# First loads and last norm of a two-layer encoder kernel: pieces alternated, a product halved, six multiplications moved to GpSimd

## The chip, the cores and the metric

The kernel runs on one core of one Trainium2 chip. The metric is the device time of one execution in microseconds (us). The time before is the median of 3 runs. A profile of one execution goes with it. The engines are named as in the profile: PE (TensorE; PEld is its weight load), DVE (VectorE), ACT (ScalarE), POOL (GpSimd) and SP (SyncE, which only issues transfers here). A q behind an engine's name is its queue of transfers.

## What is computed

The reference is a two-layer encoder on 512 tokens of width 1024. Each layer adds a half-weighted SwiGLU network, then two gated mixers (neighbourhood attention and a Fourier mix), then a second half-weighted SwiGLU network; a final RMSNorm ends it.

```
def rms_norm(x, g):
    y = xf * lax.rsqrt(jnp.mean(xf * xf, axis=-1, keepdims=True) + RMS_EPS)
    return y * g

def swiglu(x, w_in, w_out):
    g, u = jnp.split(x @ w_in, 2, axis=-1)
    return (jax.nn.silu(g) * u) @ w_out

for l in range(DEPTH):
    x = x + 0.5 * swiglu(rms_norm(x, ffn1_norm[l]), ffn1_w_in[l], ffn1_w_out[l])
    x = x + mixer(rms_norm(x, mix_norm[l]), ...)
    x = x + 0.5 * swiglu(rms_norm(x, ffn2_norm[l]), ffn2_w_in[l], ffn2_w_out[l])
return rms_norm(x, final_norm)
```

All values are float32. The change touches the start of the first SwiGLU network and the end: the last product of the last network, the addition to x, and the final norm.

## The kernel before

**Products.** Each float32 operand is split into a high part (type fp32r, which PE multiplies) and a low remainder. ACT makes the high part of a weight granule (`whi`, 128x1024 or 128x512, line 181 or 176) from the raw weights in `raw`; DVE makes the low part as `raw - whi` (`wlo`, line 184 or 177). The activations are split in the same way (`xh`, `xl`, lines 298 to 302). A product is then three matmuls, high by high, high by low, and low by high; `late_low` (lines 449 to 456) issues the two that need `whi` first and the one that needs `wlo` behind them. Matrix products are blocked in the manner of Strassen: seven products of sums of quarters instead of eight, so `at`, `xr` and some `raw` tiles are sums made on DVE (lines 166, 603 to 610, 658).

**Order of work.** The weights come as a stream of granules of up to 512 KB each, `Stream` and `Item`, which are loaded some 8 ahead and split 2 ahead (`AHEAD`). A tile scheduler puts the instructions of each engine into an order at build time; regions under `manual_schedule` keep the written order on the engines they name. Each engine runs its own queue in order and waits at semaphores.

**The start** (lines 1501 to 1518). ACT's queue loads the norm gains (`gn`, 128x48). SP's queue loads x, transposed, in parts of one, one, two, two and two k-tiles of 128x512 (`xt`), and after each part the weight granule that goes with it, the first in two halves. `Norm.given` (line 342) splits a k-tile: ACT multiplies x by its gain into `xh` (line 301), DVE makes `xl` (line 302) and an unsplit copy `xr` in two halves (line 350). Before that, PE runs 9 warm-up matmuls (line 138) on a tile that was set to zero by DVE, and of which ACT's tanh writes one column (line 135; it also loads ACT's table). The first network's product without Strassen, `plain` (lines 560 to 572), accumulates four banks `cl` over 8 k-tiles, 12 matmuls each, and product A follows it.

**The end** (lines 820 to 933). The last network's output product has steps (m, c): m the Strassen product, c the part of the inner dimension. `update` (line 664) adds a finished bank `o` (PSUM) to a 128x512 half of x: x has four row blocks `tb` 0 to 3 with two halves `i` each. `squares` sums the squares of a half on ACT (line 335). Product 4 comes last; its final step is issued by block (`by_block`), the rows of `tb` 0 first, and within a block granule after granule in the order of `late_low`. The update with bank 1 for `tb` 0 and 1, half 1, is issued after step (4, 1). The rest of the end is written out by hand for DVE and ACT, and stands behind the last `wlo`: `inverses(2)` makes 1/sqrt of the mean square for `tb` 2 and 3 in one go, `inverse` for `tb` 0 and 1 apiece (an ACT square root, and one Newton step on DVE). `gained` (line 920) multiplies a half of x by the final gains `gf` into `o` on DVE, `scaled` (line 925) multiplies the 1024 columns of a row block by its inverse on ACT and sends them out on SP's queue, and `whole` (line 932) does both for one half in one DVE instruction.

Of the kernel before, what the change touches and what calls it, by code (L numbers as in the profile page):

```python
# [17 lines left out]
P = 128  # L18
# [9 lines left out]
EPS = 1e-6  # L28
NEG = -1.0e30
WARM = 9  # L30
# [62 lines left out]
def encoder_kernel(  # L93
    ctx: ExitStack, tc: tile.TileContext, xin, xtr, wst, gains, gfin, gbias, rpb, dft, chan, mask, ident_in, rot, out
# [40 lines left out]
    S.activation(warm[:, 0:1], ones, AF.Tanh)  # L135
# [5 lines left out]
    class Raw:  # L141
# [3 lines left out]
        def load(self, parts=1):  # L145
            if self.t is None:
                self.t = raw_pool[0](self.n)
                for c in range(0, self.n, self.n // parts):
                    cs = slice(c, c + self.n // parts)
                    nc.sync.dma_start(out=self.t[:, cs], in_=wst[GRAN_AT[self.key]][:, cs])  # L150
                if self.plus:
                    G.dma_start(out=self.t, in_=wst[GRAN_AT[self.plus]][:, 0 : self.n], accum_op=ALU.add)  # L152

    class Item:
        def __init__(self, raw, add=None, neg=False, stage=0, parts=1, pieces=1, then=None):
            self.raw, self.add, self.neg, self.stage, self.parts = raw, add, neg, stage, parts
            self.pieces, self.then = pieces, then

        def load(self):
            self.raw.load(self.pieces)  # L160
            if self.add:
                self.add.load()
# [6 lines left out]
        def prep(self, nxt):  # L169
            n = self.raw.n  # L170
            hi = wp.tile([P, 1024], F32R, tag="whi", name=nm("whi"), bufs=3)[:, 0:n]
            lo = wp.tile([P, 1024], F32R, tag="wlo", name=nm("wlo"), bufs=3)[:, 0:n]
            t = self.raw.t
# [4 lines left out]
            else:  # L178
                for c in range(0, n, n // self.parts):
                    cs = slice(c, c + n // self.parts)  # L180
                    S.activation(hi[:, cs], t[:, cs], AF.Copy)  # L181
                    if nxt:
                        nxt.summed()
                    self.last = V.tensor_tensor(lo[:, cs], t[:, cs], hi[:, cs].bitcast(F32), ALU.subtract)  # L184
            if self.then:
                G.dma_start(out=t, in_=wst[GRAN_AT[self.then]][:, 0:n], accum_op=ALU.add)
            self.out = (hi, lo)

    def stage_items():
# [34 lines left out]
        def ffn(s):  # L224
            first = not items
            if first:
                for g in range(4):
                    add(Raw((s, "cl", g)), parts=2 if g < 2 else 1, pieces=2 if g == 0 else 1)
# [89 lines left out]
    class Norm:  # L318
# [23 lines left out]
        def given(self, i, k, src):  # L342

            self.tiles(i)
            g = self.gain(4 * i + k)
            split(self.h[i][:, k, :], self.l[i][:, k, :], src, g)
# [37 lines left out]
        def terms(self, tb):  # L384

            e, f = small("e", 1), small("ef", 1)
            V.tensor_scalar(e, self.ssq[:, tb : tb + 1], 1.0 / D, EPS, ALU.mult, ALU.add)
            V.tensor_scalar(f, e, -0.5, None, ALU.mult)
            return e, f

        def inverse(self, tb, e, f):

            b = self.ssq[:, 4 + tb : 5 + tb]
            q, mh, r, t = small("sq", 1), small("mh", 1), small("inv", 1), small("rt", 1)
            self.inv[tb] = r
            S.activation(q, b, AF.Sqrt, scale=1.0 / D, bias=e)
            yield
            V.tensor_scalar(mh, b, -0.5 / D, f, ALU.mult, ALU.add)
            V.reciprocal(r, q)
            yield  # L400
            V.tensor_scalar(t, r, r, mh, ALU.mult, ALU.mult)
            V.tensor_scalar(r, t, 1.5, r, ALU.add, ALU.mult)
            yield

        def inverses(self, a):

            ms, q, r, t = small("ms", 2), small("sq", 2), small("r", 2), small("rt", 2)
# [4 lines left out]
            V.tensor_scalar(ms, ms, 1.0 / D, EPS, ALU.mult, ALU.add)  # L412
            S.activation(q, ms, AF.Sqrt)
            yield
            V.reciprocal(r, q)
            yield
            V.tensor_tensor(t, r, r, ALU.mult)
            yield
            V.scalar_tensor_tensor(t, t, -0.5, ms, ALU.mult, ALU.mult)
# [1239 lines left out]
```

## Time and profile before

| what | value |
|---|---|
| median of 3 runs | 1907.28 us (1907.06 to 1907.36) |
| the profiled execution | 1906.98 us |
| its span | 1905.2 us |
| instructions in the profile | 25187 |
| granted TensorE clock, mean | 0.999 |
| busy PE / DVE / ACT / POOL | 1890.9 / 1608.4 / 1161.3 / 199.0 us |
| read from and written to HBM | 354.18 MB and 2.11 MB |

The span runs from the first to the last event of the profile, and the execution's own time is 1.78 us longer. Busy time is the sum of the instructions of an engine without double counting; a matmul's duration in the rows (0.39 us for 512 columns) contains its pipeline, so matmuls that follow each other start closer together than that. A row of the time line that ends in x2 or x3 is a group of like instructions that follow each other. A bracket at the end of a row gives how long the engine was idle before it, and what released it.

### The profile page before, as it was taken

The page shows a single profiled execution, that of the slowest core. Times are in us where ns is not written, and L with a number is a line of the kernel's source. Part 1 is how long each engine was busy: PE and PEld are TensorE (multiplying, and loading weights), DVE is VectorE, ACT ScalarE, POOL GpSimd, SP SyncE. Part 2 cuts the span into 40 slices and gives each one's busy share as a digit, 9 for nine tenths or more (in the row PEclk, how much of TensorE's full clock was granted, in tenths as well). Part 3 has the DMA queues.
Part 4 walks back from the last instruction along what each step waited for, and adds up shares of the span by engine and source line. Part 5 has one row for each costly group of instructions (what it writes and reads, how often), then busy time and mean ns, then how long its engine had stood idle before and what let it go on. Part 6 is the DMA issues. An engine that isn't in the chain of part 4 may idle for free.

```text
span 1905.2 us, 25187 instructions
## 1 busy us (share of the span) xinstructions
PE 1890.9 (99%) x9189; PEld 1586.3 (83%) x9189; DVE 1608.4 (84%) x2000; ACT 1161.3 (61%) x1676; POOL 199.0 (10%) x246
## 2 busy tenths in 40 slices
PE   9999999999999999999999999999999999999998
PEld 7888888888888888888888888888888888888886
DVE  7877899586889987889997778995769899787898
ACT  6655665467566755566665556663675566555664
POOL 0101010310111011001010100103101101000010
PEclk9999999999999999999999999999999999999999
DMA  9777499323786777649877765974147867776594
GB/s 301 204 209 184 150 254 313 100 73 99 212 217 163 174 199 205 175 154 263 245 189 212 185 178 156 277 266 129 50 121 215 211 172 173 208 177 177 171 276 144
DMA packets 104924, 361.09 MB, mean 190 GB/s; under 512 B 12064, under 2 KB 14240, under 8 KB 104800
## 3 DMA queue, kind: packets, MB, share of 16 engines
q1 hardware_dynamic: 77856, 267.42, 40.4%
q0 software_dynamic: 26800, 92.04, 27.1%
q8 instruction: 72, 1.18, 0.3%
q14 instruction: 52, 0.43, 0.1%
q10 hardware_dynamic: 144, 0.02, 0.0%
HBM read 354.18 MB, written 2.11 MB: 187 GB/s over the span
## 4 chain that ended last, share of the span: by engine, by line
PE 95%; DVE 2%; DMA 1%; ACT 1%; issue 0%; SPq 0%; DVEq 0%; ACTq 0%
PE A L453 9%; PE A L454 9%; PE A L456 9%; PE o L454 7%; PE o L453 7%; PE o L456 7%; PE ps L292 5%; PE ps L293 5%; PE ps L294 5%; PE B L453 5%; PE B L454 5%; PE B L456 5%; PE C L454 2%; PE C L453 2%; PE C L456 2%; PE tr L545 2%
## 5 line engine op out<-in xcount | busy, mean ns | idle before, releaser
L181 ACT ACTIVATE whi<-raw 128x1024 fp32r<-128x1024 f32 (+1 forms) x528 | 546.3, 1037 | 416.9 <-PE A L454 119.2
L184 DVE TENSOR_TENSOR wlo<-raw,whi 128x1024 fp32r<-128x1024 f32 (+1 forms) x528 | 630.1, 1198 | 187.3 <-ACT whi L181 185.2
L152 POOL DMA_DIRECT2D raw<-in_wst_dram x158 | 136.1, 871 | 1283.1 <-DMA raw<-in_wst_dram 631.1
L166 DVE TENSOR_TENSOR raw<-raw,raw 128x1024 f32<-128x1024 f32 (+1 forms) x146 | 172.2, 1189 | 1.2
L454 PE MATMUL A<-whi,xl 128*128 128x512 f32 x384 | 149.5, 389 | 0.0
L453 PE MATMUL A<-whi,xh 128*128 128x512 f32 x384 | 149.4, 389 | 0.0
L456 PE MATMUL A<-wlo,xh 128*128 128x512 f32 x384 | 110.5, 389 | 0.0
L176 ACT ACTIVATE whi<-raw 128x1024 fp32r<-128x1024 f32 (+1 forms) x79 | 81.8, 1035 | 36.2 <-PE A L454 9.6
L177 DVE SCALAR_TENSOR_TENSOR wlo<-raw,whi 128x1024 fp32r<-128x1024 f32 (+1 forms) x79 | 93.2, 1191 | 10.7 <-ACT whi L176 10.6
L638 ACT ACTIVATE th<-sn,rh 128x512 f32<-128x512 f32 x80 | 56.7, 714 | 69.5 <-DVE sn L527 69.5
L522 ACT ACTIVATE sn<-A 128x512 f32<-128x512 f32 x96 | 56.5, 589 | 53.5 <-PE A L456 53.5
L456 PEld LDWEIGHTS A<-wlo,xh 128*128 128x128 f32 x384 | 72.1, 188 | 15.0
L454 PEld LDWEIGHTS A<-whi,xl 128*128 128x128 f32 x384 | 72.1, 188 | 14.8
L453 PEld LDWEIGHTS A<-whi,xh 128*128 128x128 f32 x384 | 72.1, 188 | 14.8
L453 PE MATMUL B<-whi,t1h 128*128 128x512 f32 x192 | 76.2, 397 | 0.0
L453 PE MATMUL A<-whi,t3h 128*128 128x512 f32 x192 | 75.2, 392 | 0.0
L453 PE MATMUL C<-whi,xh 128*128 128x512 f32 x192 | 74.9, 390 | 0.0
L453 PE MATMUL A<-whi,t2h 128*128 128x512 f32 x192 | 74.9, 390 | 0.0
L454 PE MATMUL B<-whi,t1l 128*128 128x512 f32 x192 | 74.8, 390 | 0.0
L454 PE MATMUL A<-whi,t3l 128*128 128x512 f32 x192 | 74.8, 390 | 0.0
L454 PE MATMUL C<-whi,xl 128*128 128x512 f32 x192 | 74.7, 389 | 0.0
L454 PE MATMUL A<-whi,t2l 128*128 128x512 f32 x192 | 74.7, 389 | 0.0
(410 smaller groups left out, 4784.6 us busy)
## 6 DMA issues: line engine op xcount, KB each, us to landing
raw<-in_wst_dram SPq DMA_DIRECT2D x466, 512.0 KB
raw<-in_wst_dram POOLq DMA_DIRECT2D x162, 512.0 KB, 7.8
raw<-in_wst_dram SPq DMA_DIRECT2D x30, 256.0 KB
vs<-v SPq DMA_DIRECT2D x12, 256.0 KB
bw<-in_rpb_dram SPq DMA_DIRECT2D x32, 68.0 KB
x<-in_xin_dram SPq DMA_DIRECT2D x4, 512.0 KB
raw<-in_wst_dram POOLq DMA_DIRECT2D x8, 256.0 KB, 8.2
dft<-in_dft_dram POOLq DMA_DIRECT2D x8, 256.0 KB, 6.2
```

The source lines that it names most:

```text
L152: G.dma_start(out=self.t, in_=wst[GRAN_AT[self.plus]][:, 0 : self.n], accum_op=ALU.add)
L166: V.tensor_tensor(self.raw.t, self.raw.t, self.add.t, ALU.add)
L176: S.activation(hi, t, AF.Copy, scale=-1.0)
L177: self.last = V.scalar_tensor_tensor(lo, t, -1.0, hi.bitcast(F32), ALU.mult, ALU.subtract)
L181: S.activation(hi[:, cs], t[:, cs], AF.Copy)
L184: self.last = V.tensor_tensor(lo[:, cs], t[:, cs], hi[:, cs].bitcast(F32), ALU.subtract)
L292: PE.matmul(ps, lh, rh, start=start, stop=False, skip_group_check=again)
L293: PE.matmul(ps, lh, rl, start=False, stop=False, skip_group_check=again)
L294: PE.matmul(ps, ll, rh, start=False, stop=stop, skip_group_check=again)
L453: PE.matmul(ps, lh, rh, start=start, stop=False, skip_group_check=again)
L454: PE.matmul(ps, ll, rh, start=False, stop=False, skip_group_check=again)
L456: PE.matmul(ps, lh, rl, start=False, stop=stop, skip_group_check=again)
```

## The change

At the start:
- The gains are no array of their own any more. They stand in front of x in each row of the transposed x, and the first transfer brings the gains and the first k-tile (128x560). POOL copies them into `gn` (128x48); the first k-tile's operations take the gain from the loaded tile itself.
- The first four k-tiles of x and the first two weight granules come on SP's queue as eight transfers of about 256 KB, alternately x and weights.
- For these four k-tiles the order on DVE and ACT is written out. DVE makes the first two halves of `whi` with a copy (`tensor_copy`), ACT the next two.
- On PE, the first two k-tiles issue four high·high, then four with `xl`, then four with `wlo`. There are 10 warm-ups instead of 9; the tanh writes another tile, so they don't wait for it.

At the end:
- Six of the seven `gained` multiplications, for (2,0), (3,0), (2,1), (3,1), (0,0) and (1,0), go to POOL, issued with the load of `gf`; (0,1) stays on DVE.
- The update with bank 1 (`tb` 0 and 1, half 1) moves behind the last `wlo`, between the small steps of `inverses(2)`.
- The last granule of the last product (`tb` 1) is multiplied in two column halves of 256, 12 matmuls instead of 6, the second half into a bank of its own (`last`). The x update for it goes in three pieces of 256 columns (`quarter`).
- The sums of the final norm are regrouped: the roots are taken of the sum of squares and not of its mean, with the factor `ROOT` = 32 in the Newton step, which has fewer small instructions. The last quarter's squares are summed on DVE (`tensor_tensor_reduce`) on top of the earlier sums.
- The output for (1, 0) is scaled on ACT and sent on ACT's queue, that for (1, 1) stays on DVE and SP.

As the scheduler orders it, the low part of the weights for k-tiles 6 and 7 stands behind one more 128x1024 sum on DVE and is used by PE eight matmuls later. Some small instructions within the first 60 us change places. Between there and the end each engine's order is that of before.

```diff
-    S.activation(warm[:, 0:1], ones, AF.Tanh)
+    S.activation(sp.tile([P, 8], F32, tag="sq", name="tanh", bufs=2)[:, 0:1], ones, AF.Tanh)
...
-        def inverse(self, tb, e, f):
+        def inverse(self, tb, s, e=None):
...
-            S.activation(q, b, AF.Sqrt, scale=1.0 / D, bias=e)
+            S.activation(q, s, AF.Sqrt, **({} if e is None else {"bias": e}))
             yield
-            V.tensor_scalar(mh, b, -0.5 / D, f, ALU.mult, ALU.add)
-            V.reciprocal(r, q)
+            V.tensor_scalar(mh, s, 0.0 if e is None else e, -0.5 * ROOT, ALU.add, ALU.mult)
+            V.reciprocal(r0, q)
+            V.tensor_scalar(r, r0, r0, mh, ALU.mult, ALU.mult)
+            V.tensor_scalar(r, r, 1.5 * ROOT, r0, ALU.add, ALU.mult)
             yield
...
-        if by_block:
+        if last is not None:
             w = [ws.next() for _ in range(n)]
-            for b in range(2):
-                for i in range(n):
-                    late_low(granule(i, w[i], b), again)
+            for b, i in ((0, 0), (0, 1), (1, 0)):
+                late_low(granule(i, w[i], b), again)
+            for q in range(2):
+                z = slice(q * 256, (q + 1) * 256)
+                rest = granule(1, w[1], 1)
+                rest = [(last[:, 0:256] if q else p[:, z], lh, ll, rh[:, z], rl[:, z], q == 1 and k == 0, k == 1) for k, (p, lh, ll, rh, rl, _, _) in enumerate(rest)]
+                late_low(rest, not q)
             return
...
-            late_low(parts)
+            if kt > 1:
+                late_low(parts)
+                return
+            for ps, lh, _, rh, _, _, _ in parts:
+                PE.matmul(ps, lh, rh, start=kt == 0, stop=False)
+            for ps, _, ll, rh, _, _, _ in parts:
+                PE.matmul(ps, ll, rh, start=False, stop=False)
+            for ps, lh, _, _, rl, _, _ in parts:
+                PE.matmul(ps, lh, rl, start=False, stop=False)
...
-            if m == 4 and c == 1:
+            if m == 4 and c == 1 and not late:
                 update(ps[1], 1, 0, 1)
             if m == 4 and c == 0 and late:
                 gf[0] = slot(F32, "gf", (D,))
                 nc.sync.dma_start(out=gf[0], in_=bass.AP(tensor=gfin.tensor, offset=gfin.offset, ap=[[0, P], [1, D]]))
+                for tb, i in ((2, 0), (3, 0), (2, 1), (3, 1), (0, 0), (1, 0)):
+                    gained(G, tb, i)
...
+                    def quarter(p, q, z):
+                        v = x[:, 1, T + 256 * q : T + 256 * (q + 1)]
+                        V.scalar_tensor_tensor(v, p[:, z : z + 256], 0.25, v, ALU.mult, ALU.add)
+                        return v
+
                     ready = nxt.inverses(2)
                     next(ready)
-                    gained(2, 0)
+                    e = small("e", 2)
+                    V.tensor_scalar(e, nxt.ssq[:, 0:2], D * EPS, None, ALU.add)
                     next(ready)
-                    gained(2, 1)
+                    update(ps[1], 1, 0, 1, (0,))
+                    next(ready)
+                    update(ps[1], 1, 0, 1, (1,))
                     for _ in ready:
                         pass
-                    scaled(nxt, 2)
+                    for tb in (2, 3):
+                        scaled(nxt, tb)
                     update(ps[7], 1, 0, 1, (0,))
                     nxt.squares(1, 0, (0,))
...
+                    root = nxt.inverse(0, nxt.ssq[:, 4:5], e[:, 0:1])
+                    next(root)
+                    gained(V, 0, 1)
+                    quarter(ps[7][1], 1, 256)
+                    v = quarter(ps[7][1], 0, 0)
+                    junk = sp.tile([P, T], BF16, tag="junk", name=nm("junk"), bufs=2)
+                    sa = small("sa", 1)
+                    S.activation(junk[:, 0:256], v, AF.Square, accum_out=sa)
+                    next(root)
+                    v = quarter(last, 1, 0)
+                    e1, sb, j2 = small("e1", 1), small("sb", 1), slot(F32, "j2", (256,))
+                    V.tensor_scalar(e1, sa, e[:, 1:2], None, ALU.add)
+                    V.tensor_tensor_reduce(j2, v, v, 1.0, e1, ALU.mult, ALU.add, sb)
+                    root = nxt.inverse(1, sb)
+                    next(root)
                     scaled(nxt, 0)
-                    next(root[1])
-                    next(root[1])
-                    whole(nxt, 1, 0)
+                    next(root)
+                    o_, _, _, to = half(1, 0)
+                    S.activation(o_, o_, AF.Copy, scale=nxt.inv[1])
+                    S.dma_start(out=to, in_=o_)
                     whole(nxt, 1, 1)
...
-    S.dma_start(out=gn, in_=gains)
...
+        for kt in range(4):
+            t = slot(F32, "xt", (1024,))
+            if kt:
+                t = t[:, 0:T]
+                nc.sync.dma_start(out=t, in_=xtr[:, NG + kt * T : NG + (kt + 1) * T])
+            else:
+                first_gains = t[:, 0:NG]
+                nc.sync.dma_start(out=t[:, 0 : NG + T], in_=xtr[:, 0 : NG + T])
+                t = t[:, NG : NG + T]
+            src.append(t)
+            ws.items[kt // 2].raw.piece(kt % 2 * T, (kt % 2 + 1) * T)
+        ws.fetch(2)
+        G.tensor_copy(gn, first_gains)
+        norm.tiles(0)
+        with tc.manual_schedule(engines={mybir.EngineType.DVE, mybir.EngineType.Activation}):
+            for kt in range(4):
+                g = first_gains[:, 0:1] if kt == 0 else norm.gain(kt)
+                xh, xl, it = norm.h[0][:, kt, :], norm.l[0][:, kt, :], ws.items[kt // 2]
+                z = slice(kt % 2 * T, (kt % 2 + 1) * T)
+                t = it.raw.t[:, z]
+                if kt % 2 == 0:
+                    wh, wl = it.begin()
+                S.activation(xh, src[kt], AF.Copy, scale=g)
+                if kt == 0:
+                    norm.given_raw(0, 0, src[0], g)
+                if kt < 2:
+                    V.tensor_copy(wh[:, z], t)
+                else:
+                    S.activation(wh[:, z], t, AF.Copy)
+                V.scalar_tensor_tensor(xl, src[kt], g, xh.bitcast(F32), ALU.mult, ALU.subtract)
+                V.tensor_tensor(wl[:, z], t, wh[:, z].bitcast(F32), ALU.subtract)
+                if kt:
+                    norm.given_raw(0, kt, src[kt], g)
```

## The prediction

> **What bounds the kernel now.** I read the page first: the busy shares, then the chain of work that ended last.
>
> ```profile
> PE 1890.9 (99%) x9189; PEld 1586.3 (83%) x9189; DVE 1608.4 (84%) x2000; ACT 1161.3 (61%) x1676; POOL 199.0 (10%) x246
> PE 95%; DVE 2%; DMA 1%; ACT 1%; issue 0%; SPq 0%; DVEq 0%; ACTq 0%
> ```
>
> TensorE (PE) is busy 1890.9 of 1905.2 us. A change that leaves its matmuls as they are can win only the 14.3 us in which PE is not busy, and it can lose by making PE wait. The table by stretches says where those 14.3 us lie (columns: stretch, then busy time and count for PE, PEld, DVE, ACT, POOL, then clock, DMA share, GB/s).
>
> ```profile
> 0.00:6.00 6.00, 3.27 (x10) 1.23 (x10) 1.97 (x6) 2.73 (x4) 0.20 (x4) 1.00 0.62 178
> 6.00:21.00 15.00, 14.99 (x66) 11.89 (x64) 13.83 (x28) 10.75 (x15) 0.00 (x0) 1.00 1.02 400
> 21.00:29.00 8.00, 7.92 (x35) 6.39 (x35) 6.94 (x7) 5.42 (x12) 0.40 (x1) 1.00 1.03 405
> 29.00:60.00 31.00, 31.00 (x138) 25.42 (x137) 26.86 (x44) 22.19 (x37) 4.86 (x6) 1.00 0.88 231
> 1880.00:1896.00 16.00, 16.00 (x72) 13.14 (x70) 15.57 (x27) 9.42 (x16) 0.00 (x0) 1.00 0.05 17
> 1896.00:1905.20 9.20, 0.25 (x2) 0.00 (x0) 4.57 (x13) 3.20 (x5) 0.00 (x0) 0.73 0.52 201
> ```
>
> Some 9 us are behind the last matmul and most of the rest is before 6 us. In 1880 to 1896 PE is full, and DVE nearly so (15.57 of 16.00): there DVE feeds PE just in time. Set beside the changed kernel's order of instructions, each engine's order differs only in the first 60 us and in this end; at 29 to 60 us PE never waits, and it stays so if it comes a little earlier. So the sum has two terms, head and tail.
>
> **The head.** These are single rows of the time line (start, duration, engine, line, operation, and in brackets the idle time before it and its releaser).
>
> ```profile
> 2.73 3.59 PE L138 MATMUL ps<-warm 128*128 128x512 bf16 x9 [2.73 <-ACT warm L135]
> 4.22 0.62 DVE L350 TENSOR_SCALAR xr<-xt,gn 128x256 f32<-128x256 f32 x2 [3.05 <-DMA gn<-in_gains_dram]
> 4.85 0.61 ACT L181 ACTIVATE whi<-raw 128x512 fp32r<-128x512 f32 x1
> 4.98 0.75 DVE L302 SCALAR_TENSOR_TENSOR xl<-xt,gn,xh 128x512 fp32r<-128x512 f32 x1
> 5.65 0.68 DVE L184 TENSOR_TENSOR wlo<-raw,whi 128x512 fp32r<-128x512 f32 x1
> 5.98 0.58 PE L453 MATMUL cl<-whi,xh 128*128 128x512 f32 x1
> 6.39 0.40 PE L454 MATMUL cl<-whi,xl 128*128 128x512 f32 x1
> 6.73 0.63 ACT L181 ACTIVATE whi<-raw 128x512 fp32r<-128x512 f32 x1 [1.27 <-DMA raw<-in_wst_dram]
> 9.33 0.19 PEld L454 LDWEIGHTS cl<-whi,xl 128*128 128x128 f32 x1 [0.43 <-DVE xl L302]
> 19.99 1.21 DVE L184 TENSOR_TENSOR wlo<-raw,whi 128x1024 fp32r<-128x1024 f32 x1
> 21.26 0.30 PEld L456 LDWEIGHTS cl<-wlo,xh 128*128 128x128 f32 x2 [0.50 <-DVE wlo L184]
> ```
>
> ```profile
> L994 DVE CAST flip<-xl x16: 281/286/290, 339.4 to 1286.1; 128x256 fp32r<-128x256 f32 x16
> ```
>
> Now: the warm-up matmuls begin at 2.73 because they wait for ACT's write into their operand, and their queue delays the first product, whose row of 0.58 at 5.98 is a matmul of 0.23 that really begins at about 6.17. From there 96 matmuls of 0.2265 (21.74) and about 0.8 of stalls (0.43 at 9.33, and 0.50 at 21.26 of which part is covered) bring product A to 28.7.
>
> Changed: the warm-ups wait for nothing and end before 5.4 even with a tenth one. The gains come in x's first row, so DVE's xr need not wait for a transfer of their own (4.22); I take 4.05, between nothing and 0.25 earlier. DVE then does the xr pair (0.53), and copies the first weight half: the nearest row is the cast of 256 columns, 0.286, so about 0.55 for 512 (bounds 0.29 and the 0.61 of ACT's). That ends at 5.15 to 5.4, as ACT no longer makes this half; I take PE's start as 5.37, a gain of 0.8. The pieces alternate, so the second weight half is now the fourth transfer and not the third: it was used at 6.73; with 0.65 per 256 KB (400 GB/s) it comes at 7.4 at worst, at 6.05 at best. DVE is the head's queue: two copies 1.10, eight xl 5.32, eight xr pairs 4.24, four halves of wlo 2.42, two whole wlo 2.27 and two of the sums of 1.13 each (one of which the new order puts ahead of the wlo of k-tiles 6 and 7) are 17.6; from 4.05 that is 21.7, and with its waits 21.9 to 22.8. PE asks for that wlo at its 73rd matmul instead of its 65th: 5.37 + 72 x 0.2265 = 21.7. So a stall of 0.2 to 1.1 remains, and A begins 0.5 to 1.35 earlier. I take 0.9. The grouping into four hi·hi, four hi·lo, four lo·hi for two k-tiles costs no matmul. POOL's copy of the 128x48 gains is smaller than its 128x256 multiplication, 0.68 below, so it is done by 4.8, and only ACT's second xh waits for it, whose x lands after 5.3; I cost it at nothing, and at its excess over that landing if it is slower.
>
> **The tail: six multiplications on POOL.** First what a POOL multiplication does in this trace.
>
> ```profile
> 411.57 4.08 POOL L1106 TENSOR_TENSOR bm<-bw,msk 128x256 f32<-128x256 f32 x6 [42.05 <-DVE nmx L1138]
> 363.11 6.42 POOL L1106 TENSOR_TENSOR bm<-bw,msk 128x256 f32<-128x256 f32 x6 [2.71 <-ACT u L298]
> 357.65 2.18 DVE L184 TENSOR_TENSOR wlo<-raw,whi 128x1024 fp32r<-128x1024 f32 x1 [6.93 <-ACT whi L181]
> 363.54 3.08 DVE L299 TENSOR_TENSOR u<-ue,u 128x512 fp32r<-128x512 f32 x3
> 367.20 1.75 DVE L184 TENSOR_TENSOR wlo<-raw,whi 128x1024 fp32r<-128x1024 f32 x1
> 371.55 1.22 DVE L184 TENSOR_TENSOR wlo<-raw,whi 128x1024 fp32r<-128x1024 f32 x1 [1.47 <-ACT whi L181]
> ```
>
> Columns as above. Six of them alone take 4.08 (0.68 each), beside DVE work 6.42. The same wlo subtraction takes 1.22 alone, 1.75 and 2.18 beside POOL: 0.53 for one POOL operation of 256 columns, 0.96 where two went first. Three u subtractions take 3.08, where three of 0.60 with a tail of 0.08 would take 1.88. So a DVE operation with two SBUF inputs and a POOL one exclude each other and take turns, and one 256-wide turn of POOL costs DVE 0.53. The six of the change are 512 wide: 1.06 per turn by doubling; bounds 0.68 (a whole narrow one) and 1.36 (two whole ones).
>
> The Trainium skill, "SBUF — State Buffer", section "Who interferes with whom", says that a DVE instruction with two SBUF inputs contends with a GpSimd instruction that reads SBUF, for a port pair held for the whole instruction, while the loser fully blocks. By that rule wide operations block in proportion, which is the sum below; without it the tail would be the first rival's. The 1.75 and 2.18 agree with it.
>
> Where they fall: POOL's queue is idle in 1880 to 1896 (0.00 above), the first of the six waits only for the x update on DVE that ends at about 1881.6, the next for the one after it; the last four wait for nothing late.
>
> ```profile
> 1880.93 1.28 DVE L664 SCALAR_TENSOR_TENSOR x<-o,x 128x512 f32<-128x512 f32 x2
> 1882.13 1.22 DVE L658 TENSOR_TENSOR at<-at,at 128x1024 f32<-128x1024 f32 x1
> 1883.26 1.22 DVE L299 TENSOR_TENSOR c4l<-at,c4h 128x1024 fp32r<-128x1024 f32 x1
> 1886.67 3.49 DVE L184 TENSOR_TENSOR wlo<-raw,whi 128x1024 fp32r<-128x1024 f32 x3
> 1885.21 0.19 PEld L454 LDWEIGHTS o<-whi,c4l 128*128 128x128 f32 x1
> 1888.61 0.41 PEld L456 LDWEIGHTS o<-wlo,c4h 128*128 128x128 f32 x2
> ```
>
> From 1882.13 on DVE runs seven operations with two SBUF inputs without a gap (starts 1882.13, 1883.26, 1884.40, 1885.53, 1886.67, 1887.80, 1888.94). The first waits some 0.7 for POOL's first, and each of the next five turns adds 1.06: the delays are 0.7, 1.8, 2.8, 3.9, 4.9, 6.0, 6.0. The fifth, a wlo, was ready at 1887.80 and PE loads it at 1888.61: 0.75 of room, so PE stands 4.2. The others ask for less. DVE's last wlo ends at 1896.1 instead of 1890.1 (1886.67 and three of 1.13 plus the tail).
>
> **The rest of the tail.**
>
> ```profile
> 1893.39 1.15 ACT L925 ACTIVATE o<-o,r 128x1024 f32<-128x1024 f32 x1 [1.05 <-DVE r L421]
> 1895.63 0.61 PE L456 MATMUL o<-wlo,c4h 128*128 128x512 f32 x2
> 1896.28 0.69 DVE L664 SCALAR_TENSOR_TENSOR x<-o,x 128x512 f32<-128x512 f32 x1 [0.33 <-PE o L456]
> 1897.05 0.61 ACT L335 ACTIVATE junk<-x 128x512 bf16<-128x512 f32 x1
> 1898.82 1.15 ACT L925 ACTIVATE o<-o,inv 128x1024 f32<-128x1024 f32 x1 [0.74 <-DVE o L920]
> 1899.58 1.42 DVE L932 SCALAR_TENSOR_TENSOR o<-x,inv,gf 128x512 f32<-128x512 f32 x2
> ```
>
> ```profile
> 631.05 0.28 PE L505 MATMUL hA<-xh,whi 128*128 128x256 f32 x1
> 631.17 0.28 PE L506 MATMUL hA<-xl,whi 128*128 128x256 f32 x1
> ```
>
> The last granule: 12 matmuls of 256 columns at 0.12 are 1.44 for six of 0.2265, 1.36: PE ends 0.08 later, at 1896.32 without contention; half of the last update (0.35) can go before that end. The two updates that move behind the last wlo (the pair at 1890.07 in DVE's old order) are in the chain below, and the six multiplications leave DVE there. On DVE a chain of about 0.9 (first inverse) stands ahead of the last quarter, so this begins at 1897.2; square and sum on DVE 0.5, root 0.3, then ACT's whole scaling 1.06 beside DVE's inverse 0.8, then the last halves 0.75 and 0.55 on two engines instead of two on DVE. The last output is ready at 1900.3 instead of 1901.0, but 1 MB still goes out behind it at 0.65 per 256 KB, which bounds the gain: 0.3 (range +0.2 to -0.6).
>
> With contention the chain is: wlo end 1896.1; the first inverses with two updates between, 2.2: 1898.3; ACT's two scalings of 1.06: 1900.4; squares 0.7 and root 0.3: 1901.4; inverse 0.9: 1902.3, with PE done at 1900.5. The last quarter begins at 1902.4, 5.2 later than the 1897.2 above. The end is 5.2 - 0.3 = 4.9 later than before. So ACT and DVE's chain, not PE's stall alone, sets it.
>
> **Sum**: -0.9 head, +4.9 tail: +4.0 on the profiled 1906.98, 1910.98. The median shown, 1907.28, lies 0.3 above that execution, so I forecast 1911.3. A turn of 0.68 instead of 1.06 takes 2.1 off the last delay, 1909.2; one of 1.36 adds 1.5, 1912.8.
>
> **Rivals.**
> 1. POOL costs nothing that decides (it starts later, or takes turns in DVE's gaps): -0.9 - 0.3 gives 1906.1 by the median, faster than before. For it: the six at 411.57 ran undelayed in a stretch where DVE too had work. Against: here DVE has no gap, and five of its seven operations are the wlo and split subtractions that were delayed at 357.65, 363.54 and 367.20. It decides if DVE's delay at the fifth operation is under 0.75. Chance 0.20; with the head's range 1905.3 to 1907.
> 2. POOL keeps its turn back to back, as the 0.96 at 357.65 hints: DVE's c4l of 1883.26 is then up to 7 late (six turns of 1.2), ready at 1884.40 and loaded at 1885.21 before, so PE stands 6.2 and the end comes 6.3 later, 1912.7. Chance 0.10.
> 3. The head does not do what it says (second weight half late, DVE's queue longer): 0 instead of -0.9, with the contention: 1912.2. For it: 6.73 waited 1.27 for just that transfer. Chance 0.08.
>
> The likeliest case has 0.62, its own range 1909.2 to 1912.8. The range of all, 1905.8 to 1912.8, leaves out about a tenth on either side. A measurement of this kernel tells 0.2%, 3.8 us, from no change: the border to slower is 1911.1, just under my number. From the likeliest case 0.35 lies above it and 0.27 below, all of the first rival is within 0.2%, the second and third are above: slower 0.52, same 0.47, faster 0.01 (1903.5 is in no case's reach).
>
> **What would show it.** Head: first product matmul near 5.4, product A near 27.8. Contention: POOL's six rows between 1880 and 1895 (all times 0.9 earlier) long at about 2.2 each, DVE's wlo rows at 2.2 instead of 1.22, a wait of PE for wlo of some 4 near 1888. If these wlo rows are 1.2 long, the first rival holds. If PE waits, but the tail behind PE is shorter than 9 us, ACT's chain was not the limit and the time is nearer 1909. A second wait of PE between 29 and 60 us would make the head wrong.

## The result, and the profile after

The changed kernel takes 1914.12 us (median of 7 runs, 1912.35 to 1914.67), the kernel before 1907.31 (7 runs, 1906.68 to 1908.81). The ratio is 1.0032, with a 95% interval of 1.0021 to 1.0044: slower by 4.0 to 8.4 us, 6.8 by the medians. The forecast was 1911.3, within 1905.8 to 1912.8: the right direction and mechanism, too small a size, and a range that the result left.

The profiled execution took 1912.66, near the fastest of its seven, with a span of 1910.9. Here is its table by stretches, columns as in the prediction.

```profile
28.00:60.00 32.00, 31.97 (x141) 25.85 (x140) 27.06 (x39) 23.40 (x38) 4.68 (x6) 1.00 0.82 238
1880.00:1896.00 16.00, 12.30 (x48) 9.10 (x47) 16.00 (x11) 7.26 (x10) 12.43 (x6) 0.93 0.00 1
1896.00:1910.90 14.90, 6.53 (x32) 5.40 (x30) 7.85 (x27) 5.67 (x11) 0.00 (x0) 0.84 0.36 141
```

In 1880 to 1896 PE was busy 16.00 before and is busy 12.30 now. DVE has not one idle moment (16.00), but does 11 operations there where it did 27. POOL, idle there before, is busy 12.43. The granted clock is 0.93. The time line shows why: first POOL and DVE.

```profile
1881.97 12.43 POOL L950 TENSOR_TENSOR o<-x,gf 128x512 f32<-128x512 f32 x6 [22.71 <-DVE x L677]
1882.40 1.95 DVE L671 TENSOR_TENSOR at<-at,at 128x1024 f32<-128x1024 f32 x1
1884.28 2.31 DVE L305 TENSOR_TENSOR c4l<-at,c4h 128x1024 fp32r<-128x1024 f32 x1
1886.51 2.31 DVE L191 TENSOR_TENSOR wlo<-raw,whi 128x1024 fp32r<-128x1024 f32 x1
1888.74 2.31 DVE L305 TENSOR_TENSOR c4l<-at,c4h 128x1024 fp32r<-128x1024 f32 x1
1890.98 5.64 DVE L191 TENSOR_TENSOR wlo<-raw,whi 128x1024 fp32r<-128x1024 f32 x3
```

DVE's operations with two SBUF inputs take 2.31 where they took 1.22: one turn of POOL is 1.09, and 1.10 by the starts of two rows (1886.51 to 1888.74 is 2.23, for 1.13 before). Only the last of the seven, when POOL is through (1894.40), is short again: 5.64 is 2.2 + 2.2 + 1.2. The two x updates at 1881.20, which have one input in PSUM (1.28 for both), run beside POOL's first without delay. PE's rows in the same stretch:

```profile
1886.64 0.50 PE L454 MATMUL o<-whi,c4l 128*128 128x512 f32 x1 [1.04 <-DVE c4l L305]
1888.88 1.21 PE L456 MATMUL o<-wlo,c4h 128*128 128x512 f32 x4 [0.36 <-DVE wlo L191]
1893.31 0.73 PE L456 MATMUL o<-wlo,c4h 128*128 128x512 f32 x2 [2.30 <-DVE wlo L191]
1894.27 0.63 PE L454 MATMUL o<-whi,c4l 128*128 128x512 f32 x1
1894.69 0.63 PE L453 MATMUL o<-whi,c4h 128*128 128x512 f32 x1
1896.40 0.63 PE L453 MATMUL o<-whi,c4h 128*128 128x512 f32 x1
1896.83 0.63 PE L454 MATMUL o<-whi,c4l 128*128 128x512 f32 x1
1897.53 0.40 PE L454 MATMUL o<-whi,c4l 128*128 128x512 f32 x1
```

PE waits three times, and the weight load that stood at 1888.61 now stands at 1893.31: 4.7 later, from the same beginning (the last product's first `c4h` weight load is at 1880.9 in both traces). Behind that stands something that the prediction did not have: from 1893.9 to 1897.3 matmuls of 512 columns begin 0.43 apart, not 0.23. The trace's granted clock is 0.50 for just these 3.41 us (1893.91 to 1897.33), and 1.00 on both sides.

At the start, the lines that answer to those of before:

```profile
5.11 1.85 PE L581 MATMUL cl<-whi,xh 128*128 128x512 f32 x4
7.21 0.43 DVE L1561 CAST whi<-raw 128x512 fp32r<-128x512 f32 x1 [1.00 <-DMA raw<-in_wst_dram]
21.21 1.22 DVE L191 TENSOR_TENSOR wlo<-raw,whi 128x1024 fp32r<-128x1024 f32 x1
22.48 0.30 PEld L456 LDWEIGHTS cl<-wlo,xh 128*128 128x128 f32 x2 [0.51 <-DVE wlo L191]
39.14 0.19 PEld L453 LDWEIGHTS B<-whi,t1h 128*128 128x128 f32 x1 [0.45 <-ACT whi L188]
```

PE's first product matmul comes at 5.11 instead of some 6.17, but the first four are 0.43 apart (1.85 for four). DVE waits 1.00 for the second weight half, PE 0.51 for the wlo of k-tiles 6 and 7 (0.50 before), and then 0.45 at 39.14, where it did not wait before. Product A's first weight load is at 27.85 (28.46 before), product B's at 39.14 (39.34 before).

### The profile page after: what moved, and what is told of

Its sections match the earlier page's. It is cut to its first block, busy times and chain, and to the rows that moved or that the text cites. A ratio compares the mean times of both kernels' runs of the same rounds, so it can differ in the third digit from the quotient of the medians.

```text
span 1910.9 us, 25211 instructions
## 1 busy us (share of the span) xinstructions
PE 1895.0 (99%) x9196; PEld 1588.2 (83%) x9196; DVE 1611.1 (84%) x1998; ACT 1161.7 (61%) x1675; POOL 211.0 (11%) x253
## 4 chain that ended last, share of the span: by engine, by line
PE 92%; DVE 3%; DMA 2%; issue 2%; ACT 1%; POOL 0%; SPq 0%; DVEq 0%; ACTq 0%; POOLq 0%
PE A L453 9%; PE A L454 9%; PE A L456 9%; PE o L456 7%; PE o L453 7%; PE o L454 7%; PE ps L298 5%; PE ps L299 5%; PE ps L300 5%; PE B L453 4%; PE B L454 4%; PE B L456 4%; PE C L454 2%; PE C L453 2%; PE C L456 2%; PE tr L550 2%
## 5 line engine op out<-in xcount | busy, mean ns | idle before, releaser
L454 PE MATMUL B<-whi,xl 128*128 128x512 f32 x192 | 74.7, 389 | 0.0
```

The costliest lines, as they stand in the source:

```text
L454: PE.matmul(ps, ll, rh, start=False, stop=False, skip_group_check=again)
```

## The experiments

Since run-to-run differences in the middle are as large as some of the effects (from product B to the last product's first c4h the same instructions took 1841.2 to 1844.6 in the traces below), each trace is also read by three numbers from its weight-load and DVE rows: the start of product B; how long after the first c4h load DVE's last wlo ends ("DVE late"); and the time from that load to the end of the span ("end").

| kernel | median us (before on that chip) | ratio, 95% interval | B at | DVE late | end | half clock ahead of PE's end |
|---|---|---|---|---|---|---|
| before | 1907.31 | | 39.34 | 9.26 | 24.30 | no |
| before_again | one run, 1908.03 (1907.67) | | 39.29 | 11.40 | 25.73 | no |
| changed | 1914.12 (1907.31) | 1.0021 to 1.0044 | 39.14 | 15.71 | 29.98 | yes |
| after_again | one run, 1913.96 (1907.67) | | 39.30 | 16.20 | 30.49 | yes |
| gain_on_pool | 1913.77 (1907.81) | 1.0017 to 1.0039 | 39.35 | 14.35 | 29.69 | yes |
| tail_only | 1914.39 (1907.67) | 1.0021 to 1.0046 | 39.39 | 16.00 | 29.57 | no |
| six_on_dve | 1909.96 (1907.81) | 1.0001 to 1.0019 | 39.33 | 9.97 | 25.85 | no |
| pool_memset | 1907.55 (1907.81) | 0.9990 to 1.0007 | 39.58 | 10.42 | 24.26 | no |
| two_on_pool | 1909.95 (1907.18) | 1.0001 to 1.0019 | 39.14 | 11.70 | 26.39 | no |
| pool_late | 1909.05 (1907.67) | 0.9997 to 1.0015 | 39.57 | 9.39 | 25.25 | no |
| filler | 1915.29 (1907.81) | 1.0025 to 1.0050 | 39.20 | 16.87 | 32.05 | yes |
| filler_spread | 1913.03 (1907.18) | 1.0016 to 1.0037 | 38.91 | 17.38 | 30.90 | no |
| head_only | 1907.48 (1907.18) | 0.9992 to 1.0010 | 39.20 | 11.02 | 25.30 | no |
| head_squares | 1907.91 (1907.18) | 0.9994 to 1.0012 | 38.22 | 9.54 | 24.26 | no |

The theory: POOL's multiplications and DVE's two-input operations take turns; DVE falls behind, PE waits for it, and where a wait is long PE's clock drops as well. The rivals: the new order of the end costs by itself; any POOL work costs; or the loss comes through the start.

### The multiplications alone on POOL, and the end alone

gain_on_pool, on the kernel before:

```diff
+                for tb, i in ((2, 0), (3, 0), (2, 1), (3, 1), (0, 0)):
+                    gained(G, tb, i)
...
-                    gained(2, 0)
...
-                    gained(2, 1)
...
-                    gained(3, 0)
-                    gained(3, 1)
...
-                    gained(0, 0)
...
-                    gained(0, 1)
+                    gained(V, 0, 1)
```

> The kernel before, with one change: the five multiplications by the final gains for (2,0), (3,0), (2,1), (3,1) and (0,0) go to POOL as soon as their x is done; (0,1) stays on DVE, and loads, halves and the norm's small steps are those of before. Theory A (POOL and DVE lock each other out): five turns of 1.1 us; DVE's subtractions beside them take 2.3 instead of 1.22, PE waits in all 4 to 5 us between 1884 and 1894, and the kernel is 4.5 to 7 slower than before. Rival B (the loss in the changed kernel comes from its new order of the tail, the moved updates or the halves): subtractions of 1.2, no wait of PE, and a time within 0.7 of before.

It is 6.0 slower by the medians (3.2 to 7.4), the loss of the whole change within the intervals. Rival B falls: none of the moved updates, halves or regrouped sums is in this kernel.

tail_only has all of the change's end and the start of before (the hunks at the start undone).

> The kernel before with the change's end alone (POOL multiplications, halves, regrouped norm); the start is that of before. Theory A+D: all of the loss is here: 5 to 7.5 slower than before, DVE's subtractions beside POOL at 2.3, from the first c4h weight load to the end 29 to 32. Theory L (part of the loss comes through the start: it shifts transfers, so DVE is late already before the end): DVE's last wlo ends nearer to 14.4 after that weight load, as in the kernel with five POOL multiplications and before's start, than to the changed kernel's 15.7, and the loss is 4 to 5.

6.7 slower by the medians: the start has no visible share in the loss. DVE's last wlo came at 16.00, as in the changed kernel, so theory L, in the form that the start makes DVE late, is not supported.

### Back on DVE; POOL work that reads nothing; fewer and later operations

six_on_dve, on the changed kernel:

```diff
-                for tb, i in ((2, 0), (3, 0), (2, 1), (3, 1), (0, 0), (1, 0)):
-                    gained(G, tb, i)
...
-                    for tb in (2, 3):
-                        scaled(nxt, tb)
+                    gained(V, 2, 0)
+                    gained(V, 2, 1)
+                    scaled(nxt, 2)
+                    gained(V, 3, 0)
+                    gained(V, 3, 1)
+                    scaled(nxt, 3)
+                    gained(V, 0, 0)
+                    gained(V, 1, 0)
```

> The changed kernel, with its six POOL multiplications back on DVE behind the last wlo; all else of the change stays. Theory A: PE's waits at c4l and wlo near 1885 to 1893 go, and with them the half clock behind them; what is left is the head (about -0.6 to A, of which DMA noise takes some) and the tail (about -0.3): 0.3 to 1.2 faster than before, 6 to 7.5 faster than the changed kernel. Rival B (the tail's new order costs by itself): still 3 or more slower than before.

PE's waits and the half clock are gone, as expected, but it is not faster than before: 0.2 to 3.6 slower. The rows show the reason, a cost that I had not given this kernel.

```profile
1893.85 3.70 DVE L954 TENSOR_TENSOR o<-x,gf 128x512 f32<-128x512 f32 x6
1897.47 0.68 DVE L677 SCALAR_TENSOR_TENSOR x<-o,x 128x512 f32<-128x512 f32 x1
```

The six in a row keep DVE until 1897.5, when PE ends altogether (1897.45), and only then does DVE make the x update of row block 0, which in the kernel before stands 2.7 ahead of PE's end (1893.57 for 1896.24). From PE's last matmul to the end it takes 10.38 (8.95 before, 8.36 changed). So the multiplications are not free on DVE either, where I put them, but cost less there than on POOL beside the subtractions.

pool_memset, on the changed kernel:

```diff
-        eng.tensor_tensor(o_, v, g, ALU.mult)
+        if eng is G:
+            G.memset(o_, 1.0)
+        else:
+            V.tensor_tensor(o_, v, g, ALU.mult)
```

> The changed kernel, with POOL's six multiplications replaced by POOL fills of the same output tiles with 1.0 at the same places in its queue (left out: the product of x and the final gains for those six halves). Theory A, with the lock taken only where POOL reads SBUF: DVE's subtractions take 1.22, PE does not wait, and the time is 0 to 1.5 under before. Rival C (any POOL instruction that writes SBUF blocks DVE): they stay above 2 and the time is 3 or more above before.

The fills wait for no x and so ran some 20 us earlier, but beside operations of the same kind (four of the six are in the row):

```profile
1860.99 2.26 POOL L951 MEMSET o<- 128x512 f32 x4
```

```profile
1861.57 1.22 DVE L191 TENSOR_TENSOR wlo<-raw,whi 128x1024 fp32r<-128x1024 f32 x1
1862.70 1.22 DVE L305 TENSOR_TENSOR c3l<-at,c3h 128x1024 fp32r<-128x1024 f32 x1
```

1.22 each, no delay: rival C falls, these POOL instructions that only write don't block DVE. It is also the changed end without the contention: from PE's last matmul to the end 8.39 instead of 8.95, so the new end, with six multiplications gone from DVE, the halves and the regrouped norm together, shortens that part by 0.56. In time it is the same as before.

two_on_pool leaves (2,0) and (3,0) on POOL and puts four on DVE:

```diff
-                for tb, i in ((2, 0), (3, 0), (2, 1), (3, 1), (0, 0), (1, 0)):
+                for tb, i in ((2, 0), (3, 0)):
...
+                    gained(V, 2, 1)
...
+                    gained(V, 3, 1)
...
+                    gained(V, 0, 0)
+                    gained(V, 1, 0)
```

> The changed kernel with two of the six multiplications on POOL, (2,0) and (3,0), and the four others on DVE behind the last wlo. Theory A (each POOL operation of 512 columns costs DVE one turn of 1.1): two of DVE's subtractions take 1.9 to 2.3, the others 1.22; the last wlo ends 1.6 to 2.2 later after the first c4h weight load than with no POOL operation (9.3 before, 10.0 with all six on DVE), PE waits 0.8 to 2.2 at c4l and little behind it, the clock stays full, and from that weight load to the end it takes 25.5 to 28 (24.30 before, 29.98 changed). Rival H (one POOL operation running is enough to slow all seven): last wlo 14 or later, end 29 or more.

```profile
1882.51 1.95 DVE L671 TENSOR_TENSOR at<-at,at 128x1024 f32<-128x1024 f32 x1
1884.38 2.31 DVE L305 TENSOR_TENSOR c4l<-at,c4h 128x1024 fp32r<-128x1024 f32 x1
1886.61 1.21 DVE L191 TENSOR_TENSOR wlo<-raw,whi 128x1024 fp32r<-128x1024 f32 x1
```

Two POOL operations, two long rows on DVE, then 1.21 at once. The waits, the clock and the end are in the expected ranges (2.31 a hair above 2.3). The last wlo comes 1.73 later than with all six on DVE, as expected, but 2.45 later than before; rival H falls. The time is still 0.2 to 3.6 above before.

pool_late holds POOL back until DVE's last wlo is done (the output tiles are still taken early):

```diff
+                    G.tensor_copy(small("after", 2), e)
+                    for tb, i in ((2, 0), (2, 1), (3, 0), (3, 1), (0, 0), (1, 0)):
+                        gained(G, tb, i)
```

> The changed kernel with the six POOL multiplications held back until DVE's last wlo is done (a POOL copy of a value made behind it stands ahead of them). Theory A: the DVE operations with two SBUF inputs that fed PE are now alone: 1.22 each, PE does not wait, the clock stays full, and from the first c4h weight load to the end it takes 24 to 26.5; behind the last wlo the tiny DVE operations with two SBUF inputs (128x2) now wait up to a POOL operation each. The time is 0 to 2.5 above before. Rival B (any placing on POOL costs as much): 28 or more.

The end takes 25.25, the last wlo comes at 9.39: the place of the operations decides, not the engine as such. What they meet now is small, but no less blocked:

```profile
1895.30 1.22 DVE L419 SCALAR_TENSOR_TENSOR rt<-rt,ms 128x2 f32<-128x2 f32 x1
1896.55 1.22 DVE L421 SCALAR_TENSOR_TENSOR rt<-rt,r 128x2 f32<-128x2 f32 x1
1897.69 0.68 DVE L677 SCALAR_TENSOR_TENSOR x<-o,x 128x512 f32<-128x512 f32 x1
```

Operations on 128x2 elements, 0.16 before, take 1.22 with two SBUF inputs, while the x update of 128x512, of the same kind but with one input in PSUM, takes its 0.68 beside POOL. (POOL's six took 7.97, 1.3 each.)

### The half clock

filler, on the changed kernel, was meant to keep PE busy in its longest wait, but its matmuls stand one granule too late, so they added work:

```diff
+        for _ in range(FILL if fill is not None else 0):
+            PE.matmul(fill, parts[0][1], parts[0][3], start=True, stop=True)
         for ps, lh, _, _, rl, _, stop in parts:
...
```

> The changed kernel with 11 extra matmuls of 512 columns into the still unused bank, placed in PE's queue just ahead of the wlo that PE waits for longest (2.73 us at 1893.31). They fill some 2.5 us of that wait and cost at most 0.2 of their own. Theory D (the wait makes the chip drop PE's clock to half for 3.4 us after it): the clock stays at 1.00 between 1893 and 1900, matmuls there are 0.23 and not 0.43 apart, PE ends 1.5 to 1.8 earlier, and the time falls by 0.5 to 2 against the changed kernel, since DVE and ACT's chain takes over. Rival E (the slow spacing has another cause, PE waiting for each low part): spacing and time unchanged within 0.3.

It doesn't test D as meant: in this trace DVE was later, the longest wait was at the first c4l (2.20, ahead of the filler), and the half clock followed that one, from 1887.70 to 1891.11. filler_spread has the same lines with 5, 3 and 8 matmuls in front of the three waits.

> The changed kernel with extra matmuls into the still unused bank in all three places where PE waits near the end: 5 ahead of the first c4l, 3 ahead of the first wlo and 8 ahead of the second wlo that it waits for (the earlier filler stood one granule too late and only added work). They take up waiting that is there anyhow. Theory D (PE's clock drops to half for 3.41 because it stood still for some 2.7 just before): clock 1.00 from 1885 to the last matmul, matmuls 0.23 apart throughout, PE's end 0.8 to 1.7 sooner after the first c4h weight load than the changed kernel's 21.62, and the end up to 1 sooner than its 29.98. Rival E: a stretch of 3.41 at half clock behind the waits as in the changed kernel.

```profile
1884.00:1900.00 16.00, 14.02 (x60) 10.91 (x59) 15.97 (x16) 5.40 (x9) 12.01 (x6) 1.00 0.00 0
```

The granted clock stays 1.00 (0.89 in the changed kernel for the same stretch), which agrees with theory D but doesn't show it. On the grid of 3.41 us that the last section reads from the traces, the boundaries here are 1886.88, 1890.29 and 1893.71; without the extra matmuls I estimate from the rows at most 1.5 us of waiting within any one step, and no step with so little was followed by half the clock in any trace. What carries theory D, and not rival E, is the granted clock itself and the comparison of all traces there.

The times did not follow: DVE was 1.67 later than in the changed kernel's trace, so PE ended at 21.69 after the c4h load (21.62) and the end came at 30.90, not sooner. From the load for the last long-awaited wlo to PE's end it took 7.6 instead of 9.2, 1.6 less, about the 1.7 that half a clock over 3.41 us costs PE. What that is worth in time is seen with DVE's lateness taken out. From DVE's last wlo to the end it took 14.3 in both traces of the changed kernel; 13.6 in tail_only, which kept its full clock with PE waiting as long (2.33); and 13.5 in filler_spread. So some 0.7 of the loss is the half clock; the rest of its 1.7 is hidden behind ACT's and DVE's chain.

### The start

head_only is the kernel before with the hunks of the start (loads, DVE's copies, the grouping on PE, the warm-ups). head_squares has one more change:

```diff
+            norm.squares(0, 0)
+            norm.squares(1, 0)
             with tc.manual_schedule(engines={mybir.EngineType.DVE, mybir.EngineType.Activation}):
...
-                norm.squares(0, 0)
-                norm.squares(1, 0)
```

> The kernel before with the change's start alone; the tail is that of before. Theory F (the start wins 0.6 at product A, and most of it is given back at 38.5, where PE waits for a whi that ACT makes late because three sums of squares moved behind a whi that waits for PE): product A begins 0.5 to 0.7 earlier than before's 28.46, product B only 0.1 to 0.3 earlier than 39.34, and the time is within 1 of before. Rival G (the start is worth the forecast 0.9 and the loss of it in the changed kernel was noise): B begins 0.8 to 1.0 earlier.

> As the kernel with the change's start alone, but the two first pairs of sums of squares are issued ahead of the region with a written order, so that ACT makes t3h before them. Theory F: no wait of PE at 38.5, product B begins 0.5 to 0.7 earlier than before's 39.34; the time is up to 1 under before. Rival G: no difference to the kernel with the start alone.

head_only: A at 27.91 (0.55 earlier), B at 39.20 (0.14 earlier), time the same as before. Theory F holds. ACT's rows show the cause, first before, then changed:

```profile
25.71 1.06 ACT L176 ACTIVATE whi<-raw 128x1024 fp32r<-128x1024 f32 x1 [2.58 <-PE cl L454]
26.68 1.04 ACT L298 ACTIVATE t3h<-xr 128x1024 fp32r<-128x1024 f32 x1
```

```profile
25.15 1.06 ACT L185 ACTIVATE whi<-raw 128x1024 fp32r<-128x1024 f32 x1 [3.89 <-issue]
26.11 0.62 ACT L341 ACTIVATE junk<-x 128x512 bf16<-128x512 f32 x1
27.34 0.62 ACT L341 ACTIVATE junk<-x 128x512 bf16<-128x512 f32 x1
27.96 1.05 ACT L304 ACTIVATE t3h<-xr 128x1024 fp32r<-128x1024 f32 x1
```

ACT stands idle for 3.89 before a whi, which in the kernel before waits for PE's reads of its buffer (in the changed kernel's row the bracket names no releaser); three of the four sums of squares, which before ran ahead of that whi, now queue behind it. t3h begins at 27.96 instead of 26.68, all that follows is as late, and PE waits 0.45 for the whi of product B. In head_squares the wait at 39 is gone and B begins at 38.22, 1.12 earlier, more than expected; A is 1.12 earlier as well (27.34), since PE did not wait at 22.5 either: the second weight half was there sooner (DVE's cast of it waited 0.31 and began at 6.61; 1.21 and 7.27 in head_only), and DVE's later work is as much earlier. Why that transfer came sooner is not shown, so what the moved squares themselves gain is the 0.45 of PE's wait. Its trace is the shortest of all (span 1904.5), but its median is 1907.91 against 1907.18: no gain that the runs can show. So no run here shows that an earlier product B makes this kernel faster, and no version that beats the kernel before came out.

### Once more, the same two kernels

> The kernel before once more, for a second trace of it: theory L (run to run, transfers near 1848 come early or late by about 1.4 and leave DVE behind PE) has the last wlo end between 9.2 and 11 after the first c4h weight load and the stretch between B and that load vary by up to 2; if both repeat within 0.1 (9.26 and 1841.56), the spread seen in the other kernels comes from their changed start.

> The changed kernel once more, for a second trace: theory L+D has PE's longest wait, the place of the half clock and the length of the end move with DVE's lateness: DVE's last wlo 15.0 to 17.5 after the first c4h weight load and the end 29 to 32.5; a repeat within 0.1 of 15.71 and 29.98 would mean that the spread of its times (1912.35 to 1914.67) comes from elsewhere.

The kernel before, unchanged, has DVE 2.1 later in the second trace (11.40, a little beyond the 11 expected), and then PE waits in it, too:

```profile
1886.30 0.19 PEld L454 LDWEIGHTS o<-whi,c4l 128*128 128x128 f32 x1 [1.51 <-DVE c4l L299]
```

In that trace DVE sat idle 1.50 at 1849.39 for a whi, which was not so in the first. DVE has little room to catch up near the end (busy 15.57 of 16.00 before), so how late it is differs from run to run, before as after (15.71 and 16.20). So theory L holds as run-to-run spread, and not as an effect of the start.

## Why the prediction was right or wrong

**Likeliest case, the mechanism: right.** POOL's six and DVE's seven take turns, at the place and in the order given. A turn is 1.09 to 1.10 where I took 1.06, and the delay of the last wlo is 6.45 in the first traces (9.26 to 15.71) where I had 6.0. The fifth operation held PE longest, as said. Its weight load came 4.7 later for my 4.2. The Trainium skill, "SBUF — State Buffer", section "Who interferes with whom", on which I leaned for the step from 256 to 512 columns, agrees with the runs in both halves: two-input operations are blocked for most of a POOL instruction (1.09 of the 1.3 that one takes in pool_late, down to a 128x2 operation), and a POOL instruction that only writes blocks nothing (1.22 beside fills).

**The head, -0.9: a term that was mis-sized; the first traces give -0.2.** A came 0.6 earlier, inside the bounds of 0.5 to 1.35, and DVE's wlo that holds it ended at 22.43, inside 21.9 to 22.8. That PE's slow first four matmuls cost nothing is seen in two_on_pool, whose clock was full from 4.17 on and whose A began at 27.86 all the same. But B is only 0.2 earlier. The step that failed is the sentence that PE never waits from 29 to 60 us "and it stays so if it comes a little earlier": that would hold if all engines came earlier too, and ACT came 1.3 later, so PE waited 0.45. ACT's order of instructions showed the squares moved; I counted that as small.

**The tail, +4.9: 5.7 in the first traces.** The new end without the contention (pool_memset) is 0.6 shorter behind PE's last matmul, for my 0.3. Against that stand the turns, 0.45 more in all, and a term that was not in the sum at all, the second step that failed: the half clock after PE's wait, 1.7 us of PE and some 0.7 of the end. The chain behind the wait was therefore PE's, and not ACT's and DVE's alone, as the prediction had it with PE done at 1900.5 (it ended at 1902.53): in the chain of work (start, duration, what) DVE's x update follows PE's first column half and not a scaling of ACT.

```profile
1901.57 0.25 PE o L456 x2
1901.83 0.02 issue
1901.85 0.76 DVE x L895 x2
```

**The sum.** By the two first traces -0.2 at B, +0.2 in the middle and +5.7 at the end make the 5.7 by which the spans differ (1910.9 and 1905.2), where I had +4.0. The medians differ by 6.8; the profiled execution is one of the fastest of its seven, and the last 1.1 is not attributed to a cause. So of the 2.8 by which the forecast of 1911.3 fell short, 0.7 is the head, 0.8 the tail with its half clock, 0.2 the middle, and 1.1 stays open.

**The range.** Its upper end, 1912.8, was the sum with the widest POOL turn, on before's median. I took the three runs shown, 0.3 apart, as the spread. Single runs of the kernel before lie between 1905.6 and 1911.4 on other chips, and its two traces differ by 2.1 in DVE's lateness. In the changed kernel's two traces the end moves with that lateness one for one (16.20 for 15.71, 30.49 for 29.98). Neither that spread nor the clock was in the bounds.

**Rivals.** The first (POOL costs nothing that decides, 1906.1) is refuted for this kernel; its time is nearly that of pool_memset, where POOL reads nothing. The second (POOL keeps its turn back to back) did not occur: the rows alternate strictly. The third had the start's share about right.

## What to carry to other kernels

Before work moves from a full DVE to an idle POOL, look at what DVE does at that time: if it runs operations with two SBUF inputs and POOL reads SBUF, each moved operation costs DVE a turn of POOL (1.1 us for 128x512), more than the 0.6 that it took on DVE. Ask of a shortened stage not only whether the next stage is free of waits, but which instructions were put behind a waiting one on each engine. And when PE is made to wait for some 2 us near the end, add the half clock that may follow, and count run-to-run lateness of the engine that feeds it as part of the range.

## What the runs showed of the hardware

PE's clock moves in steps of 3.41 us. In the changed kernel the trace gives full clock for 1887.57, half for 3.41 and full for 10.24, in other traces 1880.74 and 1894.40: all whole multiples of 3.413. It dropped after a wait that filled more than half of one such step and not after an equally long one that fell across two. In filler 2.20 of the step ending at 1887.70 were waited, and it dropped; in tail_only the wait of 2.33 ending at 1895.74 lay across the boundary at 1894.91 (1.5 and 0.8), and it did not. All 14 traces agree: if each is cut into such steps from where its full clock begins, every full-clock step in which PE, by its matmul rows, stands idle for 1.91 us or more is followed by half the clock (2.00 in gain_on_pool, 2.20 in filler, 2.30 in the changed kernel, 1.91 in after_again behind its last matmul), and none with 1.76 or less is (1.76 in tail_only behind its last matmul).

```profile
1895.74 0.74 PE L449 MATMUL o<-wlo,c4h 128*128 128x512 f32 x2 [2.33 <-DVE wlo L185]
1896.32 0.40 PE L446 MATMUL o<-whi,c4h 128*128 128x512 f32 x1
1896.55 0.40 PE L447 MATMUL o<-whi,c4l 128*128 128x512 f32 x1
```

The Trainium skill, "TensorE: Matmul & The Clock Gate", section "Part 1: The HAM clock gate (the "warmup" mystery)", describes a free-running window of 3413 ns, which the traces show; the section "HAM oscillation — how this bites in real kernels" warns of idle gaps longer than about 3.4 us. Here 1.9 to 2.3 us were enough where they fell into one window, so the measurement goes further than the rule. The same grid makes an earlier warm-up no sure gain: the warm-ups began 1.5 us earlier (1.22 for 2.73), and the full clock came at 4.17 to 7.13 in the ten traces with the changed start, and at 5.59 to 7.35 in the four with the start of before.
